# A hybrid decoder block: who issues the first small loads, and who sums the mixer's shift and scale

## The chip, the cores and the metric

The kernel runs on one core of a Trainium2 chip. The metric is device time in microseconds (us) of one execution. A core has five engines that run their own instruction streams in order: TensorE (PE, with its weight loads as PEld), VectorE (DVE), ScalarE (ACT), GpSimd (POOL) and SyncE (SP). Transfers between device memory and on-chip memory are issued by an engine's queue and carried out by 16 DMA engines.

## The reference

A decoder block over 2048 tokens of width 1024, all in float32. Cut to what matters here:

```
mod = c @ w_ada + b_ada                       # c: 1024 numbers, w_ada: 1024 x 6144
shift_m, scale_m, gate_m, shift_f, scale_f, gate_f = split(mod, 6)
h = rms_norm(x, g_pre_mix) * (1 + scale_m) + shift_m
proj = h @ w_in                               # q|k|v of attention, q|k|v|o, i|f of the mLSTM, gates
...                                           # sliding-window attention, chunkwise mLSTM, merge, w_out
x = x + gate_m * rms_norm(mix, g_post_mix)
...                                           # the same sandwich around a SwiGLU FFN
```

So nothing of the large products can start before the first columns of shift_m and scale_m (two products of the vector c with 1024 x 1024 matrices, 8 MB to read) are there.

## The kernel before

**Tiling.** The mixer goes over the sequence in four blocks of 512 tokens; the FFN follows in two halves. h is kept transposed: eight tiles k of 128 features by 512 tokens, each as a hi and a lo part (`hhi`, `hlo`), because each float32 product is made of three products in a faster format, hi·hi, hi·lo and lo·hi (`mm3`). Weights are loaded raw, 1 MB at a time (`raw`, two buffers), and each *piece* of a weight is split by `split`: ScalarE casts the hi part (`whi`, L256), VectorE subtracts to get the lo part (`wlo`, L257). The split tiles have four buffers, that is two pieces. `run` goes through a list of items; behind each piece it calls `advance`, which loads the next raw tile and splits pieces up to two ahead.

**Order.** The program is traced in one order. A planner then orders the instructions of each engine by a simulated timeline, by readiness and traced order, so an engine's final order may differ from the traced one. `tc.keep_in_program_order(i)` pins an instruction behind the one traced before it on its engine; `tc.issue_after(i)` puts what is traced inside it behind `i` on `i`'s engine. Neither adds a wait for another engine. Transfers wait for one of eight semaphores used in turn.

**The start.** SyncE issues x (two loads of 1 MB, `load_x`, L115), ten small loads (L142 to L153: biases, gains, convolution weights, positions, c, sinks), and w_ada in four chunks of 256 columns for shift and for scale (`load_ada`, L126, four loads of 512 KB for each chunk). Chunk 0 stands ahead of the first raw tile of the q weights (L288), chunks 1 and 2 ahead of the second, chunk 3 ahead of the k and v weights (L718). `hprep` squares x on ScalarE (L490), takes a root, scales x (L495 on ScalarE for the first block, L497 on VectorE for the others), and then, feature tile by feature tile, has TensorE transpose it (L209) and ScalarE write `hhi` (L504) and a copy (L506) with scale `s1` and bias `sh1`; GpSimd makes `hlo` (L507).

**Shift and scale.** `ada_first` handles a chunk: for each of eight k (rows p·8+k of w_ada), acc += c[k]·raw[k] on VectorE (L422 for the first k, L424 for the rest), for shift and scale; for chunk 0 the shift part is summed by TensorE instead, with c as a one-column weight. Matmuls with a column of ones (L204, `mix<-ones,tm`) sum over the partitions, and three small VectorE instructions (L444 to L446) add the bias and apply the gain. A chunk gives two feature tiles of h, which one piece of the q weights (`token_group`, four pieces of 24 products) multiplies. `rope_tables(0)` (L570 to L618, mostly VectorE) makes the tables that the rotary step behind q needs.

Of the kernel before, what the change touches and what calls it, by code (L numbers as in the profile page):

```python
# [2 lines left out]

# [1 line left out]

# [5 lines left out]
F32 = mybir.dt.float32  # L11
# [56 lines left out]
def decoder_block(ctx: ExitStack, tc: tile.TileContext, a: dict, out: bass.AP, dbg=None):  # L68
# [9 lines left out]
    small.tile([P, 8], F32, name="small_end", bufs=1)  # L78
# [24 lines left out]
    def tm(shape, dtype=F32):  # L103
        return mpool.tile(shape, dtype, tag="tm", name=nm("tm"), bufs=9)
# [8 lines left out]
    def load_x(src, big, i):  # L113
        xb = big([2, D])
        nc.sync.dma_start(xb, src[i * 256:(i + 1) * 256, :].rearrange("(t p) c -> p t c", p=P))  # L115
        return xb

    def load_ada(c0, n):

        kn = 2048 // n  # L120
        raws = {0: [], 1: []}
        for k0 in range(0, KD, 4):
            for part in (0, 1):
                if k0 % kn == 0:
                    raws[part].append(big([kn, n]))
                nc.sync.dma_start(raws[part][-1][:, k0 % kn:k0 % kn + 4, :],  # L126
                                  w_ada[:, part * D + c0:part * D + c0 + n].rearrange("(p k) c -> p k c", k=KD)[:, k0:k0 + 4, :])
# [6 lines left out]
    r0 = 0  # L134
    off = {}
# [9 lines left out]
    x_first.append(load_x(x_d, big, 1))  # L145
    posi = tm([S // P, P], I32)
    nc.sync.dma_start(posi, a["positions"].rearrange("o (t p) -> (o t) p", p=P))
    c_sb = const.tile([P, KD], F32, name="c_sb")
    nc.sync.dma_start(c_sb, a["c"].rearrange("o (p k) -> (o p) k", k=KD))
    b_if = const.tile([P, 8], F32, name="b_if")  # L150
    nc.sync.dma_start(b_if, a["b_if"].to_broadcast([P, 8]))
    sinks = const.tile([P, HQ], F32, name="sinks")
    nc.sync.dma_start(sinks, a["attn_sinks"].to_broadcast([P, HQ]))  # L153
    ada_raws = {c0: load_ada(c0, n) for c0, n, _ in ADA[:ADA_AHEAD[0]]}


    ident = const.tile([P, P], F32, name="ident")
# [38 lines left out]

    now = [0.0]
    streams = []

    def mm(o, lhsT, rhs, start, stop, resumed=False):  # L200

        n = int(np.prod(rhs.shape[1:]))
        now[0] += max(110.0, n * 0.422) if rhs.dtype == F32R else max(218.0, n * 1.7)
        T.matmul(o, lhsT=lhsT, rhs=rhs, start=start, stop=stop, skip_group_check=resumed)  # L204

    def transpose(o, i):
        now[0] += 110.0
# [36 lines left out]
    def split_tile(name):  # L244
        return wpool.tile([P, 1024], F32R, tag="split", name=nm(name), bufs=4)

    def split(src, shape, pair_heads=False, eng=V):
        n = int(np.prod(shape))
        hi, lo = split_tile("whi"), split_tile("wlo")
        hv = hi[:, :n].rearrange("p (k c) -> p k c", k=shape[0])  # L250
        lv = lo[:, :n].rearrange("p (k c) -> p k c", k=shape[0])
        if pair_heads:
            for k in range(shape[0]):
                sv = src[:, k, :].rearrange("p (g j d) -> p g j d", g=HKV, d=HD)
                hk, lk = (v[:, k, :].rearrange("p (j g d) -> p g j d", g=HKV, d=HD) for v in (hv, lv))
                A.copy(hk, sv)  # L256
                V.tensor_tensor(lk, sv, hk.bitcast(F32), op=ALU.subtract)  # L257
# [9 lines left out]
    class Piece:  # L267
        def __init__(self, raw, view, shape, mms, pair_heads=False):
            self.raw, self.view, self.shape, self.mms, self.pair_heads = raw, view, shape, mms, pair_heads
            self.wt = None  # L270
            raw.left += 1

    def mm3(ps, l, r, first, last):
# [68 lines left out]
    def run(items, between):  # L342
# [11 lines left out]
        def advance():  # L354
            nonlocal nload, nsplit
            while True:
                alive = sum(1 for r in raws[max(0, nload - 3):nload] if r.left)
                if nload < len(raws) and alive < 2:
                    between.get(nload, lambda: None)()
                    raws[nload].tile = raws[nload].load()  # L360
                    nload += 1
                    continue
                if nsplit < len(pieces) and nsplit < done + 2 and pieces[nsplit].raw.tile is not None:
                    p = pieces[nsplit]
                    p.wt = split(p.view(p.raw.tile), p.shape, p.pair_heads, G if nsplit < 3 else V)
                    p.raw.left -= 1
                    nsplit += 1
                    continue
                return

        advance()
        for it in items:
            if not isinstance(it, Piece):
                it()
                continue
            for _ in it.mms(it.wt):
                tick()
            tick()
            done += 1
            advance()  # L380
# [3 lines left out]
    s2 = const.tile([P, KD], F32, name="s2")  # L384
    b1 = const.tile([P, 48], F32, name="b1")
    V.tensor_scalar(b1, cols[:, off["b_ada"]:off["b_ada"] + 48], 1.0, None, op0=ALU.add)
    sh1 = const.tile([P, KD], F32, name="sh1")
    sh2 = const.tile([P, KD], F32, name="sh2")
    gg_m = mpool.tile([P, D], F32, name="gg_m")
# [33 lines left out]
            else:  # L423
                V.scalar_tensor_tensor(acc, raw[:, k, :], c_, acc, op0=ALU.mult, op1=ALU.add)  # L424

    def ada_first(c0, n, raws, on_pe):

        t0, nt = c0 // P, n // P
        acc = [tm([P, n]) for _ in range(2)]
        pt = mix_tile()  # L430
        ps = {part: mix_tile() for part in on_pe}
        for k in range(KD):
            for part in (0, 1):
                if part in on_pe:
                    mm(ps[part][0:1, :n], c_sb[:, k:k + 1], raws[part][k], k == 0, k == KD - 1)
                else:
                    ada_terms(acc[part], raws[part][k].unsqueeze(1), k, 1)
        for part in on_pe:
            A.copy(acc[part][0:1, :], ps[part][0:1, :n])
        for part in (0, 1):  # L440
            r = 1 if part in on_pe else P
            for j in range(nt):
                mm(pt[:, part * 8 + j:part * 8 + j + 1], acc[part][:r, j * P:(j + 1) * P], ones[:r, 0:1], True, True)
        V.tensor_tensor(sh1[:, t0:t0 + nt], pt[:, :nt], col("b_ada", t0, nt), op=ALU.add)  # L444
        V.tensor_tensor(s1[:, t0:t0 + nt], pt[:, 8:8 + nt], b1[:, 8 + t0:8 + t0 + nt], op=ALU.add)
        V.tensor_tensor(s1[:, t0:t0 + nt], s1[:, t0:t0 + nt], col("g_pre_mix", t0, nt), op=ALU.mult)  # L446

    def ada_stream(parts, gap):
        for part, kind in parts:
# [27 lines left out]
    def hprep(key, src, big, s_c, sh_c, first=False):  # L477
# [6 lines left out]
        for i in range(2):  # L484
# [6 lines left out]
            V.tensor_tensor(ss[:, 0:2], ss[:, 0:2], ss[:, 2:4], op=ALU.add)  # L491
            r = rsqrt_of_sumsq(ss[:, 0:2], 2)
            for t in range(2):
                if first:
                    A.activation(xb[:, t, :], xb[:, t, :], AF.Copy, scale=r[:, t:t + 1])  # L495
                else:
                    V.tensor_scalar(xb[:, t, :], xb[:, t, :], r[:, t:t + 1], None, op0=ALU.mult)  # L497
                xs.append(xb[:, t, :])
        yield L_X
        for k in range(KD):  # L500
# [145 lines left out]
    tables = {}  # L646

    def first_h(c0, n, on_pe):
        ada_first(c0, n, ada_raws[c0], on_pe)
        for _ in range(n // P):  # L650
            next(hp0)

    w_ba = a["w_branch_attn"][0]
# [2 lines left out]
    def block(b):  # L656
# [58 lines left out]

        def load_kv():
            raw = raw_tile([KD, 264])
            nc.sync.dma_start(raw[:, :, :256], w_in[:, C_K:C_K + 256].rearrange("(k p) c -> p k c", p=P))  # L718
# [960 lines left out]
```

## Time and profile before

| | |
|---|---|
| median of 3 runs | 2771.63 us (2771.41 to 2775.72) |
| profiled execution | 2771.54 us, span 2769.8 us |
| mean granted TensorE clock | 0.994 |
| PE busy | 2704.9 us (98%) |
| DVE busy | 1922.7 us (69%) |
| ACT busy | 1233.1 us (45%) |
| DMA | 402.63 MB, mean 145 GB/s |

Times in the profile count from the span's start. A row of the timeline has the start, the duration, engine, line, operation, what is written and read, and in brackets how long the engine had been idle and what ended that. A row of the waits has the waiter, the releaser, the sum, the number of times and the longest. A row of the windows has, for a stretch, its length, the busy time and the number of instructions of each engine, the granted TensorE clock, the DMA engines' busy share and the GB/s.

### The profile page before, as it was taken

To read this page: it belongs to the slowest core of one execution; us is meant where nothing else is said; L and a number is where in the kernel's file an instruction comes from. 1 tells how busy PE (TensorE), PEld (TensorE's weight loads), DVE (VectorE), ACT (ScalarE), POOL (GpSimd) and SP (SyncE) were. 2 spreads that over 40 slices of the span, in tenths; PEclk is the share of its full clock that TensorE was granted. 3 is DMA by queue.
4 is the path that set the end of the run, shared out by engine and by line. 5 is a ranking of instruction groups with operands and counts; after the bars stand their busy time and mean duration, and the time that the engine had idled before them with its cause. 6 is when DMAs were issued, how large, how long until landed. Compare 5 with 4: busy or idle time off the path is not lost.

```text
span 2769.8 us, 35110 instructions
## 1 busy us (share of the span) xinstructions
PE 2704.9 (98%) x12654; PEld 2199.7 (79%) x12654; DVE 1922.7 (69%) x3802; ACT 1233.1 (45%) x2285; POOL 153.1 (6%) x201
## 2 busy tenths in 40 slices
PE   6999999999999999999999999999999999999998
PEld 4778878788877888768887888887777888888886
DVE  7768657587674876657776777776676767666456
ACT  4543365433554335544363343334554333333444
POOL 2100001001010010110100000000000000000000
PEclk9999999999999999999999999999999999999999
DMA  7233353242552424523356555545666333233566
GB/s 236 88 111 103 100 180 123 80 137 80 169 163 65 135 86 139 180 67 97 98 168 216 172 176 181 175 152 194 203 236 210 130 102 108 98 111 131 189 212 213
DMA packets 280533, 402.63 MB, mean 145 GB/s; under 512 B 19220, under 2 KB 176536, under 8 KB 280360
## 3 DMA queue, kind: packets, MB, share of 16 engines
q1 hardware_dynamic: 280360, 400.40, 44.3%
q8 instruction: 99, 1.62, 0.2%
q14 instruction: 74, 0.61, 0.1%
HBM read 320.62 MB, written 79.73 MB: 145 GB/s over the span
## 4 chain that ended last, share of the span: by engine, by line
PE 87%; DVE 5%; DMA 4%; ACT 2%; issue 1%; POOL 0%; SPq 0%; DVEq 0%; POOLq 0%; ACTq 0%
PE acc L204 63%; PE mix L204 22%; PE mix L209 2%; DVE hl L1121 1%; DMA raw<-in_w_ffn_down_dram 1%; DVE tm L424 1%; DMA tx<-in_w_ada_dram 0%; ACT hl L1120 0%; DMA raw<-in_w_ffn_gate_dram 0%; DMA raw<-in_w_in_dram 0%; DMA raw<-as_d 0%; DMA x1n<-tx 0%; ACT big L1222 0%; POOL rs L472 0%; DMA w<-x 0%
## 5 line engine op out<-in xcount | busy, mean ns | idle before, releaser
L1120 ACT CAST hl<-raw 128x512 fp32r<-128x512 f32 x564 | 337.1, 620 | 400.2 <-PE mix L204 173.3
L1121 DVE TENSOR_TENSOR hl<-raw,hl 128x512 fp32r<-128x512 f32 x564 | 377.1, 687 | 169.5 <-ACT hl L1120 167.0
L259 ACT CAST whi<-raw 128x1024 fp32r<-128x1024 f32 (+1 forms) x208 | 212.1, 1020 | 501.0 <-PE acc L204 439.1
L260 DVE TENSOR_TENSOR wlo<-raw,whi 128x1024 fp32r<-128x1024 f32 (+1 forms) x208 | 247.4, 1189 | 181.0 <-ACT whi L259 178.2
L204 PE MATMUL acc<-hhi,wlo 128*128 128x512 f32 x896 | 353.9, 395 | 0.0
L204 PE MATMUL acc<-hhi,whi 128*128 128x512 f32 x896 | 352.4, 393 | 0.0
L204 PE MATMUL acc<-hlo,whi 128*128 128x512 f32 x896 | 351.8, 393 | 0.0
L204 PE MATMUL acc<-big,hl 128*128 128x512 f32 x1056 | 254.0, 389 | 0.6 <-ACT w L1328 0.6
L204 PE MATMUL acc<-hl,hl 128*128 128x512 f32 x1008 | 237.0, 393 | 6.9 <-DVE hl L1121 4.3
L204 PEld LDWEIGHTS acc<-big,hl 128*128 128x128 f32 x1056 | 198.0, 188 | 42.3 <-ACT w L1328 1.1
L204 PEld LDWEIGHTS acc<-hl,hl 128*128 128x128 f32 x1008 | 187.1, 188 | 52.6 <-DVE hl L1121 9.5
L204 PEld LDWEIGHTS acc<-hhi,wlo 128*128 128x128 f32 x896 | 168.3, 188 | 42.4 <-issue 8.1
L204 PE MATMUL mix<-big,hl 128*128 128x512 f32 x704 | 197.6, 392 | 3.2 <-DVE big L1257 3.2
L204 PEld LDWEIGHTS acc<-hlo,whi 128*128 128x128 f32 x896 | 168.3, 188 | 37.8 <-issue 3.2
L204 PEld LDWEIGHTS acc<-hhi,whi 128*128 128x128 f32 x896 | 168.4, 188 | 37.2 <-issue 4.1
L204 PE MATMUL mix<-hl,hl 128*128 128x512 f32 x792 | 182.4, 390 | 2.0 <-ACT hl L1120 1.3
L204 PEld LDWEIGHTS mix<-hl,hl 128*128 128x128 f32 x792 | 148.0, 188 | 35.5 <-DVE hl L1121 2.7
L204 PE MATMUL acc<-whi,big 128*128 128x512 f32 x512 | 166.0, 396 | 0.0
L204 PE MATMUL acc<-big,whi 128*128 128x512 f32 x512 | 158.4, 394 | 0.0
L204 PEld LDWEIGHTS mix<-big,hl 128*128 128x128 f32 x704 | 132.9, 189 | 32.0 <-DVE big L1257 4.4
L204 PE MATMUL acc<-whi,hhi 128*128 128x512 f32 (+1 forms) x384 | 133.3, 373 | 22.1 <-DVE tx L530 8.9
L204 PE MATMUL acc<-wlo,hhi 128*128 128x512 f32 (+1 forms) x384 | 140.7, 370 | 2.6 <-DVE wlo L260 2.6
(335 smaller groups left out, 4746.6 us busy)
## 6 DMA issues: line engine op xcount, KB each, us to landing
raw<-in_w_in_dram SPq DMA_DIRECT2D x76, 1024.0 KB, 5.1
as_d<-w SPq DMA_DIRECT2D x154, 256.0 KB, 2.2
raw<-as_d SPq DMA_DIRECT2D x70, 512.0 KB, 3.5
raw<-in_w_ffn_gate_dram SPq DMA_DIRECT2D x22, 1024.0 KB, 5.3
raw<-in_w_ffn_up_dram SPq DMA_DIRECT2D x22, 1024.0 KB, 6.3
raw<-ws_d SPq DMA_DIRECT2D x40, 512.0 KB, 4.3
tx<-in_w_ada_dram SPq DMA_DIRECT2D x64, 256.0 KB, 3.1
raw<-in_w_out_dram SPq DMA_DIRECT2D x16, 1024.0 KB, 5.1
```

Of the source, the lines that this page charges most:

```text
L204: T.matmul(o, lhsT=lhsT, rhs=rhs, start=start, stop=stop, skip_group_check=resumed)
L209: T.transpose(o, i, ident[:k, :k])
L259: A.copy(hv, src)
L260: V.tensor_tensor(lv, src, hv.bitcast(F32), op=ALU.subtract)
L424: V.scalar_tensor_tensor(acc, raw[:, k, :], c_, acc, op0=ALU.mult, op1=ALU.add)
L1120: A.copy(v(hi), src)
L1121: V.tensor_tensor(v(lo), src, v(hi).bitcast(F32), op=ALU.subtract)
```

## The change

- The ten small loads move from SyncE's to ScalarE's queue, c first; SyncE issues x, x, and chunk 0 at once.
- `ADA` now names, for each chunk, the k whose terms TensorE sums: all eight for chunk 0, k = 0 and 1 for the others. TensorE takes the raw w_ada tile as the weight and a column of c as the moving operand, so the result falls straight into the column that the partition sum goes to. VectorE sums k = 2 to 7 of chunks 1 to 3 (`ada_sums`), and the matmul with ones adds that to the same column.
- The bias and the gain are applied by ScalarE: two activations for each 128 columns, with `b1g` = (1 + b)·g made once.
- Chunk i + 1's matmuls and its two feature tiles are traced inside piece i, behind its sixth of eight `mm3` (a hook), and pinned there; the next product is queued behind the last of them. Chunks 2's and 3's VectorE sums are traced behind the piece before and pinned.
- For the first block x is scaled by VectorE too. The rope tables are traced behind chunk 3.

```diff
-ADA = [(0, 256, (0,)), (256, 256, ()), (512, 256, ()), (768, 256, ())]
+ADA = [(0, 256, tuple(range(8))), (256, 256, (0, 1)), (512, 256, (0, 1)), (768, 256, (0, 1))]
...
-    x_first = [load_x(x_d, big, 0)]
+    x_first = [load_x(x_d, big, i) for i in range(2)]
+    ada_raws = {c0: load_ada(c0, n) for c0, n, _ in ADA[:ADA_AHEAD[0]]}
+    c_sb = const.tile([P, KD], F32, name="c_sb")
+    nc.scalar.dma_start(c_sb, a["c"].rearrange("o (p k) -> (o p) k", k=KD))
...
-        nc.sync.dma_start(stack[r0:r0 + n, :], v)
+        nc.scalar.dma_start(stack[r0:r0 + n, :], v)
...
+    behind = []
     def mm(o, lhsT, rhs, start, stop, resumed=False):
...
-        T.matmul(o, lhsT=lhsT, rhs=rhs, start=start, stop=stop, skip_group_check=resumed)
+        with tc.issue_after(behind.pop().ins) if behind else nullcontext():
+            return T.matmul(o, lhsT=lhsT, rhs=rhs, start=start, stop=stop, skip_group_check=resumed)
...
-            for _ in it.mms(it.wt):
+            for n, _ in enumerate(it.mms(it.wt)):
                 tick()
+                if n == it.hook[0]:
+                    it.hook[1]()
...
+    def ada_sums(c0, n, on_pe):
+        rest = [k for k in range(KD) if k not in on_pe]
+        if not rest:
+            return
+        acc = ada_acc[c0] = [tm([P, n]) for _ in range(2)]
+        for k in rest:
+            for part in (0, 1):
+                c_, w_ = c_sb[:, k:k + 1], ada_raws[c0][part][k]
+                if k == rest[0]:
+                    i = V.tensor_scalar(acc[part], w_, c_, None, op0=ALU.mult)
+                else:
+                    i = V.scalar_tensor_tensor(acc[part], w_, c_, acc[part], op0=ALU.mult, op1=ALU.add)
+                if c0 > ADA[1][0]:
+                    tc.keep_in_program_order(i)
+    def ada_first(c0, n, on_pe):
+        t0, nt = c0 // P, n // P
+        acc = ada_acc.get(c0)
         pt = mix_tile()
...
+        for part, k in sorted(((part, k) for k in on_pe for part in (0, 1)), key=lambda z: (z[1] // 4, z)):
             for j in range(nt):
+                i = mm(pt[:, part * 8 + j:part * 8 + j + 1], ada_raws[c0][part][k][:, j * P:(j + 1) * P], c_sb[:, k:k + 1],
+                       first, k == KD - 1, resumed=True)
+                first = False
+                if c0:
+                    tc.keep_in_program_order(i)
+        if acc:
+            for j in range(nt):
+                for part in (0, 1):
+                    i = tc.keep_in_program_order(mm(pt[:, part * 8 + j:part * 8 + j + 1], acc[part][:, j * P:(j + 1) * P],
+                                                    ones[:, 0:1], False, True, resumed=True))
+            behind[:] = [i]
+        for j in range(nt):
+            t = t0 + j
+            A.activation(sh1[:, t:t + 1], pt[:, j:j + 1], AF.Identity, bias=col("b_ada", t))
+            A.activation(s1[:, t:t + 1], pt[:, 8 + j:9 + j], AF.Identity, scale=col("g_pre_mix", t), bias=b1g[:, t:t + 1])
+            yield
...
-                if first:
-                    A.activation(xb[:, t, :], xb[:, t, :], AF.Copy, scale=r[:, t:t + 1])
-                else:
-                    V.tensor_scalar(xb[:, t, :], xb[:, t, :], r[:, t:t + 1], None, op0=ALU.mult)
+                V.tensor_scalar(xb[:, t, :], xb[:, t, :], r[:, t:t + 1], None, op0=ALU.mult)
...
     def program():
-        for i, ch in enumerate(ADA):
-            if i == 3:
+        items = [it for b in range(NBLK) for it in block(b)]
+        yield lambda: ada_sums(*ADA[1])
+        yield lambda: first_h(*ADA[0])
+        for i in range(len(ADA)):
+            if i + 1 < len(ADA):
+                if i:
+                    yield lambda ch=ADA[i + 1]: ada_sums(*ch)
+                items[0].hook = 5, lambda ch=ADA[i + 1]: first_h(*ch)
+            else:
                 yield lambda: tables.update({0: rope_tables(0)})
-            yield lambda ch=ch: first_h(*ch)
-        items = [it for b in range(NBLK) for it in block(b)]
+            yield items.pop(0)
```

Two small pins are left out above: the first two pieces' lo parts are queued behind `b1g` on VectorE, and the first load of the k and v weights behind the last load of w_ada.

More of the change, by code (lines that the diff above doesn't have):

```diff
@@ L1 @@
 import math
-from contextlib import ExitStack
+from contextlib import ExitStack, nullcontext
 import numpy as np
@@ L77, in decoder_block @@
     small = ctx.enter_context(tc.tile_pool(name="small", bufs=2))
-    small.tile([P, 8], F32, name="small_end", bufs=1)
     wpool = ctx.enter_context(tc.tile_pool(name="wpool", bufs=2))
@@ L141, in decoder_block @@
                        ("norm_w", a["mlstm_norm_w"].rearrange("o (t p) -> (o t) p", p=P), 4)):
-        nc.sync.dma_start(stack[r0:r0 + n, :], v)
+        nc.scalar.dma_start(stack[r0:r0 + n, :], v)
         off[name] = r0
         r0 += n
-    x_first.append(load_x(x_d, big, 1))
     posi = tm([S // P, P], I32)
-    nc.sync.dma_start(posi, a["positions"].rearrange("o (t p) -> (o t) p", p=P))
-    c_sb = const.tile([P, KD], F32, name="c_sb")
-    nc.sync.dma_start(c_sb, a["c"].rearrange("o (p k) -> (o p) k", k=KD))
+    nc.scalar.dma_start(posi, a["positions"].rearrange("o (t p) -> (o t) p", p=P))
     b_if = const.tile([P, 8], F32, name="b_if")
-    nc.sync.dma_start(b_if, a["b_if"].to_broadcast([P, 8]))
+    nc.scalar.dma_start(b_if, a["b_if"].to_broadcast([P, 8]))
     sinks = const.tile([P, HQ], F32, name="sinks")
-    nc.sync.dma_start(sinks, a["attn_sinks"].to_broadcast([P, HQ]))
-    ada_raws = {c0: load_ada(c0, n) for c0, n, _ in ADA[:ADA_AHEAD[0]]}
+    nc.scalar.dma_start(sinks, a["attn_sinks"].to_broadcast([P, HQ]))
     ident = const.tile([P, P], F32, name="ident")
@@ L245, in split_tile, with split @@
         return wpool.tile([P, 1024], F32R, tag="split", name=nm(name), bufs=4)
-    def split(src, shape, pair_heads=False, eng=V):
+    def split(src, shape, pair_heads=False, first=False):
         n = int(np.prod(shape))
@@ L256, in split @@
                 A.copy(hk, sv)
-                V.tensor_tensor(lk, sv, hk.bitcast(F32), op=ALU.subtract)
+                with tc.issue_after(b1g_made.ins) if first else nullcontext():
+                    V.tensor_tensor(lk, sv, hk.bitcast(F32), op=ALU.subtract)
         else:
@@ L364, in advance @@
                     p = pieces[nsplit]
-                    p.wt = split(p.view(p.raw.tile), p.shape, p.pair_heads, G if nsplit < 3 else V)
+                    p.wt = split(p.view(p.raw.tile), p.shape, p.pair_heads, nsplit < 2)
                     p.raw.left -= 1
@@ L386, in decoder_block @@
     V.tensor_scalar(b1, cols[:, off["b_ada"]:off["b_ada"] + 48], 1.0, None, op0=ALU.add)
+    b1g = small.tile([P, KD], F32, name="b1g", bufs=1)
+    b1g_made = V.tensor_tensor(b1g, b1[:, 8:16], cols[:, off["g_pre_mix"]:off["g_pre_mix"] + KD], op=ALU.mult)
     sh1 = const.tile([P, KD], F32, name="sh1")
@@ L648, in first_h @@
     def first_h(c0, n, on_pe):
-        ada_first(c0, n, ada_raws[c0], on_pe)
-        for _ in range(n // P):
+        for _ in ada_first(c0, n, on_pe):
             next(hp0)
```

32 lines of the change are left out of this document (9 added, 23 removed).

## The prediction

> **What bounds the kernel now.** I read the spans first, then the windows, the waits, the timeline and chain of the first 90 us, and the DMA view. The windows decide where to look:
>
> ```profile
> core 0: 2769.8 us, clock 0.994
> core 0: us, PE busy (x) PEld busy (x) DVE busy (x) ACT busy (x) POOL busy (x), PEclk, DMA share, GB/s
> 0.00:24.70 24.70, 8.28 (x34) 3.92 (x34) 10.34 (x36) 13.88 (x28) 3.89 (x45) 1.00 0.88 293
> 24.70:57.60 32.90, 26.18 (x120) 21.06 (x120) 32.42 (x83) 10.41 (x17) 8.16 (x6) 0.84 0.71 228
> 57.60:65.00 7.40, 7.36 (x24) 5.53 (x24) 6.57 (x16) 3.36 (x6) 2.57 (x2) 0.77 0.36 116
> 65.00:77.00 12.00, 10.47 (x78) 9.50 (x78) 11.77 (x30) 6.16 (x11) 0.00 (x0) 1.00 0.33 100
> 77.00:90.00 13.00, 11.61 (x70) 10.04 (x68) 10.07 (x42) 7.40 (x16) 1.29 (x4) 1.00 0.55 183
> 90.00:2769.80 2679.80, 2641.02 (x12334) 2149.68 (x12332) 1851.49 (x3599) 1191.85 (x2210) 137.14 (x144) 1.00 0.44 143
> ```
>
> Behind 90 us TensorE is busy 2641.02 of 2679.80 us at full clock: what it gains in front, it keeps to the end. In front it is idle 16.4 us up to its first product at 24.7, then 6.7, 0.0, 1.5 and 1.4 us, and from 24.7 to 65 the granted clock is 0.84 and 0.77. Between 24.7 and 57.6 VectorE is full (32.42 of 32.90). The waits and the timeline say what TensorE waited for:
>
> ```profile
> ACT hhi L504 <- DVE s L446: 22.8, 4, 10.6
> PE acc L204 <- ACT hhi L504: 8.6, 3, 3.2
> 21.41 2.18 ACT L256 CAST whi<-raw 128x512 fp32r<-128x512 f32 x4 [1.21 <-DMA raw<-in_w_in_dram]
> 24.75 0.54 PE L204 MATMUL acc<-whi,hhi 128*128 128x512 f32 x1 [2.53 <-ACT hhi L504]
> 38.09 0.79 PE L204 MATMUL acc<-whi,hhi 128*128 128x512 f32 x1 [3.24 <-ACT hhi L504]
> 53.00 0.50 PE L204 MATMUL mix<-ones,tm 128*128 128x1 f32 x4
> 56.23 0.15 DVE L444 TENSOR_TENSOR sh<-mix,cols 128x2 f32<-128x2 f32 x1
> 56.81 0.78 ACT L504 ACTIVATE hhi<-mix,sh,s 128x512 fp32r<-128x512 f32 x1 [6.55 <-DVE s L446]
> 57.64 0.50 PE L204 MATMUL acc<-whi,hhi 128*128 128x512 f32 x1 [2.87 <-ACT hhi L504]
> ```
>
> Each h chunk waits for VectorE: for its 16 sums, and then for its three small finishing operations in VectorE's queue. For the last chunk TensorE's partition sums are through at 53.5, and L444 comes at 56.23. The last piece of the q projection starts at 57.64.
>
> **The loads.** The queue's issues, and the DMA rates in slices of 1.5 us:
>
> ```profile
> 0.80 1.28 ACT L490 ACT_TABLE_LOAD   x1 [0.80 <-PEq L1669]
> 0.80 4.85 DMA big<-in_x_dram
> 6.97 0.43 SPq L153 DMA_DIRECT2D sinks<-in_attn_sinks_dram  x1
> 7.44 2.89 SPq L126 DMA_DIRECT2D big<-in_w_ada_dram  x4
> 8.68 0.63 ACT L490 ACTIVATE tx<-big 128x512 f32<-128x512 f32 x1 [0.45 <-DMA big<-in_x_dram]
> 10.38 11.01 DMA raw<-in_w_in_dram
> GB/s 0 131 421 367 404 123 51 290 355 367 355 378 378 353 348 348 349 347 348 348 360 378 375 354 348 348 350 355 223 26 0 0 0 0 0 0 113 378 208 0
> ```
>
> From 12 us on, the pipe is full at about 350 GB/s, hence 6.0 us for a chunk's 2.1 MB and 3.0 us for half of the q weights; between 7.5 and 10.5 us (123, 51) it is nearly empty, because chunk 0 was issued only at 7.44, behind ten small loads. Off SyncE, chunk 0 follows x: x by 8.7 as now, chunk 0 by 14.7, the first q weights by 17.7 instead of 21.4. That is 3.7 us; the hole's missing bytes alone (227+299 GB/s over 1.5 us each, by 350) give 2.3, the moved issue 5.6: these are its bounds. The estimated landings, before and after: chunk 1 27.4, 23.7; chunk 2 33.4, 29.7; second q weights 36.4, 32.7; chunk 3 42.4, 38.7. ScalarE pays ten issues of 0.43, 4.7 us with their gaps, ahead of squares that start at 5.67, when x has landed. With its table load of 1.28 it is free at 6.8, late by 1.1 us; I cost it at nothing, since x is ready by 14 to 15 and chunk 0's sums are later.
>
> **Prices.** The rows for the pieces that follow:
>
> ```profile
> 6.21 0.19 ACT L490 ACTIVATION_READ_ACCUMULATOR tx<-big 128x1 f32 x1
> 11.15 4.25 ACT L495 ACTIVATE big<-big,rs 128x1024 f32<-128x1024 f32 x4
> L497 DVE TENSOR_SCALAR big<-big,rs x12: 746/748/754, 352.6 to 1071.8; 128x1024 f32<-128x1024 f32 x12
> 21.71 0.50 PE L204 MATMUL mix<-ones,tm 128*128 128x1 f32 x4
> 32.87 1.07 PE L209 MATMUL mix<-ident,big 128*128 128x128 f32 x8
> 33.33 2.85 DVE L424 SCALAR_TENSOR_TENSOR tm<-big,c_sb,tm 128x256 f32<-128x256 f32 x7
> 22.06 0.69 DVE L257 TENSOR_TENSOR wlo<-raw,whi 128x512 fp32r<-128x512 f32 x1 [1.32 <-ACT whi L256]
> 25.09 0.63 PE L204 MATMUL acc<-wlo,hhi 128*128 128x512 f32 x1
> 25.51 0.63 PE L204 MATMUL acc<-whi,hhi 128*128 128x512 f32 x1
> 31.04 1.07 PE L204 MATMUL acc<-whi,hlo 128*128 128x512 f32 x4
> 38.79 1.57 DVE L424 SCALAR_TENSOR_TENSOR tm<-big,c_sb,tm 128x256 f32<-128x256 f32 x1
> 47.05 0.28 DVE L570 TENSOR_TENSOR tx<-inv_freq,pos 128x128 f32<-128x128 f32 x1
> 65.69 0.29 DVE L614 SCALAR_TENSOR_TENSOR tx<-tx 128x128 f32<-128x128 f32 x1
> ```
>
> A one-column matmul with 128 weight columns costs 0.13 us (four in 0.50), a transpose 0.13, a VectorE sum 0.41, a weight's hi part 0.55 (four in 2.18), its lo part 0.6 at the pitch of that engine. A product starts every 0.23 us warm and every 0.42 (25.09 to 25.51) at half clock. The new small ScalarE finish is bounded by the 0.19 and the 0.78 rows; I take 0.25, near the 128x1 row, so 0.5 for the two that a transposed chunk waits for. VectorE's x scaling costs 4 times 0.75, while ScalarE loses 4.25 us; x is then ready between 14 and 15.
>
> **The change, step by step.**
>
> Chunk 0: no VectorE sums. When the last quarter lands at 14.7, 8 matmuls remain (1.0), then 0.5 and one h tile (0.78): 17.0. The q weights at 17.7 plus a cast make the first product 18.4, against 24.75. TensorE has then waited 2.6 us; the trace shows half clock behind waits of 2.53 and 2.87, so I charge 8 products at 0.42 and 10 at 0.23: 5.7, to 24.1. The Trainium skill ("TensorE: Matmul & The Clock Gate", What's actually happening) has the clock fall only after an idle window of about 3.4 us; by that this piece would be 1.5 us shorter, but the trace's waits were under it and still paid.
>
> Chunk 1, inside piece 0 behind 18 of 24 products: it landed at 23.7, and 7 of the 12 remaining sums need the last quarter: 2.9, to 26.6. TensorE's eight matmuls end at 25.1; it waits 1.5, sums 0.5. Then 6 products and 8 transposes (2.4) cover ScalarE's 1.3: piece 1 at 29.5, against 38.09.
>
> Chunk 2: the program traces the split of piece 2's weights ahead of these sums and pins the first sum behind it. So they start after the second q weights, 32.7, two casts 1.1 and a lo part 0.6: 34.4, though their data is there at 29.7. Twelve sums are 4.9, plus one hold of 1.1 (1.57 against about 0.48 while GpSimd works on hlo): 40.4. TensorE is at the pinned matmuls at 33.7, done with eight at 34.7, and waits 5.7: half clock again. Sums to 40.9, then 6 products at 0.42 and the transposes: piece 2 at 44.4.
>
> Chunk 3: piece 3's split needs piece 1's two weight buffers, free at 43.4; two casts and a lo part, 45.1; sums with a hold, 51.1. TensorE comes at 48.5, ends its eight at 49.5, waits 1.6, and starts piece 3 at 54.0 instead of 57.64: 3.6 us. The piece then runs warm, 5.6 against 7.4 us: 1.8 more, 5.4 at the end of q.
>
> The rope tables (35 operations, L570 to L614, at some 0.25: 8.8 us) are what VectorE does in its gaps, 26.6 to 33.8 and 40.4 to 44.5; in the trace before they lie between 47 and 66, mixed with chunk 3's sums. That cover costs up to 4.7 if it is gone (below). VectorE sheds 8 + 12 sums (8.2) and 12 small finishes (about 1.2), and takes 3.0 for x: 6.4 less, so of TensorE's idle 2.9 us from 65 to 90, where VectorE is busy 11.77 of 12, I count 2.1 as gained. Together 5.4 + 2.1 = 7.5 us.
>
> The profiled execution is 2771.54 us: the span of 2769.8 and 1.7 around it; the median of the runs is 2771.63, the same. So 2771.5 − 7.5 = **2764.0 us**. Its own uncertainty is 3 us: the load hole (2.3 to 5.6) and the two half-clock windows (1.6 each).
>
> **Rivals.**
>
> *No hold on VectorE.* If piece 2's lo parts don't stand in front of chunk 2's sums, they end at 32.6, before TensorE arrives; piece 2 starts at 37.5, chunk 3's sums at 41.6, piece 3 at 45.7, q ends at 51.3, 13.7 earlier. The rope tables then have no gap and give back some 3: 11 us, 2760.5. For it: VectorE's order is a planner's, not the program's. Against: the explicit pin. Chance 0.2.
>
> *Rope tables in the wrong gap.* Placed whole between chunk 2's sums and piece 3's split, 8.8 us fill a gap of 4.1: chunk 3 is 4.7 later, piece 3 at 58.7. Of the gain only the later idle remains, with the earlier tables: some 2 us, 2769.5. For it: they float freely. Chance 0.15.
>
> *Slower: VectorE's pinned chain behind an unmoved load.* The small loads share the pipe, the hole persists in another place, and the second q weights land at 36.4 as now. Then in one string: two casts and lo 38.1, sums 44.1, rope tables with two holds 55.1, split 56.3, sums 62.3, 2.9 to the next product: 65.2 against 57.64, 7.6 slower; the saved idle gives back nothing as VectorE is later too: 2779. It decides from 60.0 on (2 us of warm clock given). Beside it: the Trainium skill ("Trainium Kernel Development and Optimization", Key Constraints) says that queues of several engines run on the same 16 DMA engines and save issue time alone; the row with 123 and 51 says that issue time was what was missing. Chance 0.1.
>
> *It doesn't reach the end:* TensorE arrives earlier at the attention of block 0 and waits there for VectorE; within 1 us of before, 2771. Chance 0.05.
>
> **How the numbers follow.** The forecast has 0.5, its own range 2761 to 2767. 0.2% is 5.5 us, about what a measurement here can tell. Faster by more: 0.82 of 0.5 and all of 0.2, 0.61. Same: 0.08 of the forecast, 0.15 and 0.05, 0.28. Slower 0.1 and a rest, 0.11. A range of 2758.5 to 2770.0 holds the first three cases and leaves out the other two and the tails.
>
> **What would show it.** First product near 18.4, piece 1 near 29.5, piece 2 near 44, piece 3 near 54; no DMA hole behind x; VectorE idle or on rope between 27 and 33; ScalarE with eight short finishes per part and no wait on VectorE's L446. Wrong if piece 2 starts before 40 or piece 3 after 57, or if squares start after 7 us because ScalarE's issues wait.

## The result: 0.7% slower, and where the profile puts it

| | before | after |
|---|---|---|
| median (runs) | 2772.54 us (6; 2771.04 to 2775.72) | 2793.7 us (6; 2790.74 to 2795.21) |
| ratio | | 1.0073 [1.006, 1.0086] |
| profiled execution, span | 2771.54, 2769.8 us | 2795.21, 2793.5 us |

The change costs 21.2 us where 7.5 were forecast as gained. The windows of the changed kernel, cut as those of before:

```profile
core 0: us, PE busy (x) PEld busy (x) DVE busy (x) ACT busy (x) POOL busy (x), PEclk, DMA share, GB/s
0.00:24.70 24.70, 1.15 (x5) 0.85 (x5) 8.46 (x28) 8.36 (x21) 3.89 (x45) 1.00 0.96 325
24.70:57.60 32.90, 32.83 (x166) 29.82 (x167) 9.79 (x24) 8.28 (x18) 5.16 (x4) 1.00 0.55 175
77.00:90.00 13.00, 5.11 (x27) 3.97 (x26) 10.71 (x37) 3.34 (x6) 0.03 (x1) 0.81 0.44 130
90.00:2793.50 2703.50, 2663.91 (x12464) 2168.85 (x12464) 1867.99 (x3660) 1202.94 (x2233) 137.74 (x148) 1.00 0.45 143
```

TensorE does almost nothing up to 24.7 us (1.15 us against 8.28 before), is then busy without a pause up to 57.6, and stands still for 7.9 us between 77 and 90. VectorE, full between 24.7 and 57.6 before, has 9.79 of 32.9 us to do. A warning for the column PEclk: this trace holds no clock record before 44.2 us, and the column reads 1.00 there; the pitch of the matmuls below says otherwise.

For the comparisons below I number the wide products (matmuls into `acc`) of TensorE in each trace, and call a *lag* by how much later than in the trace of before one of them starts; each trace is one execution. Lag of the changed kernel: +15.2 us at the first product, +15.4 at the last of the q projection (80.0 against 64.6), +21.8 at the 350th (158 against 136 us); behind that it stays between 18.3 and 23.5 to the end. So the loss has two parts: 15 us ahead of the first product and some 7 behind q.

**Ahead of the first product.** ScalarE's queue and engine in the timeline:

```profile
0.80 0.43 ACTq L134 DMA_DIRECT2D c_sb<-in_c_dram  x1
2.34 0.31 ACTq L145 DMA_DIRECT2D tm<-in_g_pre_ffn_dram  x1
6.20 0.32 ACTq L145 DMA_DIRECT2D tm<-in_conv_w_dram  x1
7.52 0.32 ACTq L149 DMA_DIRECT2D tm<-in_positions_dram  x1
11.97 0.39 ACTq L151 DMA_DIRECT2D b_if<-in_b_if_dram  x1
12.40 0.49 ACTq L153 DMA_DIRECT2D sinks<-in_attn_sinks_dram  x1
12.92 1.28 ACT L517 ACT_TABLE_LOAD   x1 [12.92 <-DMA tm<-in_positions_dram]
14.21 0.63 ACT L517 ACTIVATE tx<-big 128x512 f32<-128x512 f32 x1
```

Each issue takes 0.3 to 0.6 us, as forecast; but between the fourth and the fifth lie 3.5 us, and between the eighth and the ninth 4.1. The eight transfer semaphores go round over both queues: `conv_w` comes to the one of x's first half, which lands at 6.2, and `b_if` to that of `conv_w`. The DMA view gives `conv_w`'s time from issue to landing, and the rates of the first 60 us in slices of 1.5:

```profile
tm<-in_conv_w_dram ACTq DMA_DIRECT2D x1, 16.0 KB, 5.7
GB/s 0 98 388 423 423 358 344 341 346 370 380 280 379 355 348 349 346 348 350 369 386 359 349 92 287 378 354 335 25 11 0 0 0 0 5 0 0 0 5 0
```

16 KB need 5.7 us in a pipe that is now full of x and w_ada: no packet of ScalarE's queue starts between 6.98 and 9.92 us. (The hole at 7.5 to 10.5 us is gone, as forecast.) ScalarE waits inside its instruction stream, and its squares start at 14.21 instead of 5.67 us. What hangs on them, on VectorE and TensorE:

```profile
18.07 1.42 DVE L521 TENSOR_SCALAR big<-big,rs 128x1024 f32<-128x1024 f32 x2 [0.90 <-POOL rs L499]
21.90 0.28 DVE L181 COPY cols<-mix 128x128 f32<-128x128 f32 x1
23.73 0.21 DVE L187 CAST tm<-tm 16x128 f32<-16x128 int32 x1
24.00 0.28 PE L189 MATMUL mix<-ident,tm 16*128 16x16 f32 x1 [10.93 <-DVE tm L187]
24.21 13.81 PE L205 MATMUL mix<-c_sb,big 128*128 128x1 f32 x64
38.22 0.34 ACT L472 ACTIVATE s<-mix,b1g,cols 128x1 f32<-128x1 f32 x1
39.91 0.79 PE L205 MATMUL acc<-whi,hhi 128*128 128x512 f32 x1
46.11 1.84 PE L205 MATMUL mix<-c_sb,big 128*128 128x1 f32 x16
```

VectorE can scale x only from 18.07 on. The cast of the positions, which needs nothing of x, is behind that in its order; their transpose (L189) waits for the cast, and chunk 0's sums are behind the transpose on TensorE. They are 64 instructions, two for each float32 matmul, that start every 0.213 us, 13.8 us in all; the 16 of chunk 1, behind wide products, start every 0.112.

**Behind q.** The waits of the first 100 us, and the place itself:

```profile
DVE wlo L259 <- ACT whi L257: 28.1, 2, 23.0
PE mix L205 <- DVE tm L446: 1.3, 2, 0.9
PE acc L205 <- ACT tm L698: 8.2, 2, 7.9
```

```profile
88.78 0.23 DVE L637 TENSOR_SCALAR tx<-tx 128x128 f32<-128x128 f32 x1
89.04 0.31 ACT L641 ACTIVATE sin<-tx 128x128 f32<-128x128 f32 x1 [7.10 <-DVE tx L637]
89.68 1.05 ACT L698 COPY tm<-acc 128x512 f32<-128x512 f32 x2
90.30 0.59 PE L205 MATMUL acc<-whi,hhi 128*128 128x264 f32 x1 [7.88 <-ACT tm L698]
```

The rope tables stand behind all of VectorE's sums in its order, 70.9 to 89.3 us, although it had been idle for 23 us between 30 and 53. ScalarE's sine waits for them, q's copies out of `acc` (L698) are behind the sine, and TensorE waits for these copies until 90.3.

### The profile page after: what moved, and what is told of

Read it like the earlier page. It is cut to its first block, busy times and chain, and to the rows that moved or that the text cites. A ratio compares the mean times of both kernels' runs of the same rounds, so it can differ in the third digit from the quotient of the medians.

```text
span 2793.5 us, 35268 instructions
## 1 busy us (share of the span) xinstructions
PE 2721.1 (97%) x12742; PEld 2218.2 (79%) x12742; DVE 1908.5 (68%) x3775; ACT 1231.6 (44%) x2296; POOL 151.9 (5%) x201
## 4 chain that ended last, share of the span: by engine, by line
PE 86%; DVE 5%; DMA 4%; ACT 2%; issue 1%; POOL 0%; SPq 0%; ACTq 0%; DVEq 0%; POOLq 0%
PE acc L205 63%; PE mix L205 22%; PE mix L210 2%; DVE hl L1145 1%; DMA w<-x 1%; DMA raw<-as_d 1%; ACT hl L1144 1%; DMA raw<-in_w_ffn_gate_dram 0%; POOL rs L499 0%; DMA ws_d<-big 0%; ACT big L1246 0%; DVE w L1502 0%; DMA raw<-in_w_ffn_down_dram 0%; DVE tm L446 0%; DVE wlo L259 0%
## 5 line engine op out<-in xcount | busy, mean ns | idle before, releaser
L205 PE MATMUL acc<-hhi,wlo 128*128 128x512 f32 x896 | 353.9, 395 | 0.0
L205 PE MATMUL acc<-hhi,whi 128*128 128x512 f32 x896 | 352.5, 393 | 0.0
L205 PE MATMUL acc<-hlo,whi 128*128 128x512 f32 x896 | 352.0, 393 | 0.0
L205 PE MATMUL acc<-big,hl 128*128 128x512 f32 x1056 | 254.0, 389 | 0.8 <-ACT w L1357 0.5
L205 PE MATMUL acc<-hl,hl 128*128 128x512 f32 x1008 | 237.4, 393 | 6.6 <-DVE hl L1145 4.6
L205 PEld LDWEIGHTS acc<-big,hl 128*128 128x128 f32 x1056 | 198.0, 188 | 42.9 <-ACT w L1352 1.1
L205 PEld LDWEIGHTS acc<-hl,hl 128*128 128x128 f32 x1008 | 186.9, 188 | 52.8 <-DVE hl L1145 9.8
L205 PEld LDWEIGHTS acc<-hhi,wlo 128*128 128x128 f32 x896 | 168.3, 188 | 41.4 <-issue 7.3
L205 PE MATMUL mix<-big,hl 128*128 128x512 f32 x704 | 197.6, 392 | 2.6 <-DVE big L1281 2.6
L205 PEld LDWEIGHTS acc<-hlo,whi 128*128 128x128 f32 x896 | 168.3, 188 | 38.7 <-issue 4.1
L205 PEld LDWEIGHTS acc<-hhi,whi 128*128 128x128 f32 x896 | 168.4, 188 | 37.1 <-issue 4.1
L205 PE MATMUL mix<-hl,hl 128*128 128x512 f32 x792 | 182.5, 391 | 1.8 <-DVE ms L497 0.9
L205 PEld LDWEIGHTS mix<-hl,hl 128*128 128x128 f32 x792 | 147.7, 188 | 35.6 <-DVE hl L1145 3.1
L205 PE MATMUL acc<-whi,big 128*128 128x512 f32 x512 | 166.0, 396 | 0.0
L205 PE MATMUL acc<-big,whi 128*128 128x512 f32 x512 | 158.3, 394 | 0.0
L205 PEld LDWEIGHTS mix<-big,hl 128*128 128x128 f32 x704 | 132.8, 189 | 31.3 <-DVE big L1281 3.8
L205 PE MATMUL acc<-whi,hhi 128*128 128x512 f32 (+1 forms) x384 | 132.9, 374 | 19.6 <-ACT tm L698 10.9
L205 PE MATMUL acc<-wlo,hhi 128*128 128x512 f32 (+1 forms) x384 | 140.4, 369 | 0.2 <-DVE wlo L262 0.2
```

The source lines that it names most:

```text
L205: return T.matmul(o, lhsT=lhsT, rhs=rhs, start=start, stop=stop, skip_group_check=resumed)
```

## The experiments

Theories, as the expectations name them. **A**: ScalarE's waits on its loads delay the squares and all that follows. **B**: one-column matmuls leave TensorE at half clock, so 64 of them cost twice what was counted. **C**: the rope tables at the end of VectorE's order cost the 7.9 us behind q. **D**, as forecast: the pinned sums of chunks 2 and 3 hold pieces 2 and 3. The results, with the positions of the first product (P1) and the start of q's last one, and the lag at the 350th:

| kernel | median, us | ratio to before | P1 | q's last | lag 350 |
|---|---|---|---|---|---|
| before | 2772.2 to 2773.7 | | 24.7 | 64.6 | 0 |
| after | 2793.7 | 1.0073 [1.006, 1.0086] | 39.9 | 80.0 | +21.8 |
| b1_loads_act | 2780.31 | 1.0027 [1.0018, 1.0036] | 32.6 | 71.3 | +7.8 |
| e1_sync_loads | 2786.03 | 1.005 [1.0035, 1.0065] | 30.1 | 71.8 | +14.1 |
| e3_rope_early | 2782.3 | 1.0039 [1.0024, 1.0053] | 39.2 | 79.3 | +11.8 |
| g0_sync_rope | 2777.85 | 1.0019 [1.001, 1.0028] | 30.4 | 72.6 | +5.2 |
| e6_warm | 2797.72 | 1.0088 [1.0071, 1.0105] | 43.6 | 84.8 | +27.0 |
| g1_sync_rope_c0 | 2780.88 | 1.0025 [1.0014, 1.0035] | 25.4 | 68.4 | +2.2 |
| e4_unpin | 2792.33 | 1.0073 [1.0058, 1.0088] | 39.7 | 77.9 | +20.7 |
| h1_sync_rope_c0_unpin | 2773.48 | 1.0003 [0.9993, 1.0012] | 25.1 | 63.6 | −2.6 |
| k1_spread | 2771.74 | 0.9994 [0.9985, 1.0003] | 25.1 | 60.2 | −3.7 |
| k3_all | 2775.27 | 1.0007 [0.9998, 1.0016] | 27.1 | 62.8 | −3.3 |

**The loads, both ways.** `b1_loads_act` is the kernel before with the load part of the change alone; `e1_sync_loads` is the changed kernel with the loads back in before's order:

```diff
# e1_sync_loads (b1_loads_act is the reverse, on the kernel before)
-    x_first = [load_x(x_d, big, i) for i in range(2)]
-    ada_raws = ...
-    nc.scalar.dma_start(c_sb, ...)            # and stack, positions, b_if, sinks
+    x_first = [load_x(x_d, big, 0)]           # then stack; x's second half; positions, c, b_if, sinks
+    nc.sync.dma_start(c_sb, ...)              # all on SyncE
+    ada_raws = ...                            # behind them
```

> The kernel before with the load part of the change alone: x twice, chunk 0 and then the rest on SyncE, the ten small loads on ScalarE. Theory A: ScalarE's squares start near 14 and its scaling of x ends near 24; first product near 33 instead of 24.75; VectorE's sums, which run on meanwhile, give part of it back by the last chunk: 2 to 8 us slower than before, about 2777. Rival (the loads are harmless or help by the 3.7 us of the forecast): within 1 us of before or faster.

> The changed kernel with the ten small loads, the second load of x and chunk 0 back on SyncE in the order of before; all else as changed. Theory A (ScalarE's issues wait for semaphores whose small loads take some 5 us each to land, so the squares start at 14.2 instead of 5.7, and x, the bias columns and the position cast, behind which TensorE's first sums stand, are late): squares at 5.7, chunk 0's sums start at 14 as their data lands and take 64 times 0.213 us, first product near 29.5 instead of 39.9, time about 10 us less, 2783. Rival (the start is late because of chunk 0's sums themselves or of VectorE's order, whoever issues the loads): first product stays behind 36, time within 4 us of 2793.

```profile
11.63 1.28 ACT L489 ACT_TABLE_LOAD   x1 [11.63 <-DMA tm<-in_mlstm_norm_w_dram]
12.93 0.63 ACT L489 ACTIVATE tx<-big 128x512 f32<-128x512 f32 x1
32.57 0.80 PE L203 MATMUL acc<-whi,hhi 128*128 128x512 f32 x1 [4.16 <-ACT hhi L503]
```

That is `b1_loads_act`: squares at 12.93, the first product 7.8 us late (6.7 at q's last), the median 8.1 us above that of before in the same round of runs; 2 to 8 were expected. In `e1_sync_loads` the sums start when their data lands, and the first product comes 9.8 us earlier than in the changed kernel:

```profile
13.96 3.55 PE L206 MATMUL mix<-c_sb,big 128*128 128x1 f32 x16 [4.46 <-DMA big<-in_w_ada_dram]
18.25 10.24 PE L206 MATMUL mix<-c_sb,big 128*128 128x1 f32 x48
30.15 0.80 PE L206 MATMUL acc<-whi,hhi 128*128 128x512 f32 x1 [0.70 <-ACT hhi L529]
```

Theory A holds from both sides: the load part alone costs 8.1 us, and taking it back gives 7.7 (10 were expected). Both runs move the queue and the order of the loads together; that it is ScalarE's stream that waits is read from the rows above, and in `e1_sync_loads` the squares start at 5.88. The sums are still 13.8 us long, and the first product is 5.4 us later than before.

**The rope tables.** `e3_rope_early` traces them behind chunk 0's two tiles of h instead of behind chunk 3; `g0_sync_rope` has this and the loads on SyncE.

```diff
# e3_rope_early
         yield lambda: first_h(*ADA[0])
+        yield lambda: tables.update({0: rope_tables(0)})
...
-            else:
-                yield lambda: tables.update({0: rope_tables(0)})
```

> The changed kernel with the rope tables traced behind chunk 0's h tiles instead of behind chunk 3. Theory C (the tables, now last on VectorE before q's rotary step, hold ScalarE's sine and cosine and behind them the copies of q's PSUM banks, for which TensorE waits 7.9 us at 82): tables done before 45, TensorE's wait gone, 8 us less, 2786. Rival (the wait only moves: VectorE's splits and the sums of chunks 2 and 3 come later by as much): less than 3 us gained.

> The changed kernel with both repairs at once: small loads back on SyncE, rope tables traced behind chunk 0's h tiles. If the two causes are separate (theories A and C), their gains add: 2793.7 - 7.7 - 11.4 = 2774.6, first product near 30, TensorE's wait on the q copies under 1 us, and what is left above the kernel before (some 2 us) is chunk 0's 64 one-column matmuls. Rival: with the loads early, VectorE is busy with rope tables when chunk 1's sums come, so they only trade places: 2778 to 2782, as each repair alone.

```profile
PE acc L205 <- ACT tm L698: 0.3, 1, 0.3
```

In `e3_rope_early` the wait of 7.9 us is 0.3, and the time falls by 11.4: theory C, with a larger price than the wait alone. The clock has the rest. These are the products 109 to 130, behind the wait, in the changed kernel and then in `e3_rope_early`:

```profile
90.30:95.30 5.00, 5.00 (x22) 5.00 (x23) 5.00 (x14) 1.02 (x2) 0.00 (x0) 0.50 0.29 96
81.57:84.25 2.68, 2.68 (x24) 2.68 (x23) 2.68 (x7) 0.58 (x1) 0.00 (x0) 1.00 0.09 31
```

In the changed kernel the clock is at half from 85.2 to 95.4 us, which makes these products 2.3 us longer. The gain of `e3_rope_early` is 0.7 us at q's last product, 8.7 at the first behind the wait, 11.0 behind the half clock, and 10.0 at the 350th.

In `g0_sync_rope` both repairs give 15.9 together, 3.2 less than their sum; but before ran 1.2 us slower in its round than in that of the single repairs, and the intervals of the ratios are 2.5 us and more to each side, so that the difference is not clear of noise. Against before it is 4.4 us slower, where some 2 were expected. Its 49th product starts at 56.1, later than in `e1_sync_loads` (52.3): piece 2's lo parts, ahead of the pinned sums, waited there 4.06 us for their cast, up to 45.84, and the clock was at half from 52.7 to 59.5. The runs do not separate the two.

**One-column matmuls and the clock.** `e6_warm` puts 16 wide products into a spare bank ahead of chunk 0's sums:

```diff
# e6_warm, in ada_first
+        if c0 == 0:
+            for _ in range(16):
+                w_ = T.matmul(wps, lhsT=wt[:, :P], rhs=wt, start=True, stop=True)   # wt: a piece's hi part
+            behind[:] = [w_]
```

> The changed kernel with sixteen wide products (128x512, the first part of the q weights with itself, into a PSUM bank that nobody reads) on TensorE right in front of chunk 0's one-column sums; they add work and change no result. Theory B (one-column matmuls run at half clock because they don't raise TensorE's clock, however many follow each other): the sums start every 0.11 us instead of every 0.213, 64 of them in about 7.2 instead of 13.7 us; the sixteen cost 5 to 7 us, so that the first product comes at about the same 39 to 40, and piece 0 is warm from its start (1.5 us less): time 2792. Rival (a one-column matmul on w_ada's tiles costs 0.213 us for another reason, such as transfers into on-chip memory at the time): the pitch stays 0.21 and the time is 5 to 7 us longer.

```profile
24.12 6.57 PE L460 MATMUL mix<-whi 128*128 128x512 f32 x16
30.53 11.17 PE L206 MATMUL mix<-c_sb,big 128*128 128x1 f32 x64
```

```profile
29.80:33.20 3.40, 3.40 (x29) 3.24 (x27) 0.07 (x1) 0.00 (x0) 0.00 (x0) 1.00 1.06 373
33.20:46.90 13.70, 13.62 (x57) 12.57 (x57) 0.00 (x0) 3.68 (x8) 2.55 (x2) 0.50 0.64 198
```

The expected 7.2 us are not reached: the 64 take 11.2 instead of 13.8, the first product comes at 43.6 instead of 39 to 40, and the kernel is no faster. The windows say why. The wide products bring the clock up for 29.8 to 33.2 us; in that time TensorE does little else than one-column matmuls, and the clock goes back to 0.50 for the next 13.7, though TensorE is busy 13.62 of them (with one-column matmuls up to 41.5, then transposes, and products from 43.6 on). So a long row of one-column matmuls neither raises the clock nor keeps it. The rival, transfers at the same time, falls: the first 25 of the 64 start every 0.112 us with the DMA share at 1.06, the others every 0.213 with 0.64. The Trainium skill ("TensorE: Matmul & The Clock Gate", What's actually happening) has the gate go by how busy the array has been, and fall after an idle window of about 3.4 us; the length of the window agrees with the traces, but here it fell in a stretch that the profile counts as busy.

`g1_sync_rope_c0` shortens the sums instead: chunk 0 as the other chunks, on `g0_sync_rope`.

```diff
-ADA = [(0, 256, tuple(range(8))), ...
+ADA = [(0, 256, (0, 1)), ...
...
+        yield lambda: ada_sums(*ADA[0])
         yield lambda: ada_sums(*ADA[1])
```

> As the run before it, and chunk 0 summed as the other chunks: part k 0 and 1 by TensorE (16 one-column matmuls instead of 64), the rest by VectorE. Theory B (one-column matmuls at half clock, 0.213 us each, are what delays the first product to 30): 48 fewer are 10.2 us of TensorE, VectorE's 12 sums cost 4.9 behind the last landing, so the first product is at 25 to 26 and the time 4 us less, 2770.5. Rival (pieces behind the first are bound by weight buffers and by the pinned sums of chunks 2 and 3 on VectorE): first product earlier, the end of q the same, time within 1 us of the run before it.

The first product moves from 30.4 to 25.4 and q's end by 4.2, as expected; the lag at the 350th falls by 3.0 only, and the median does not fall (the two intervals overlap), so neither the forecast of 4 us less nor the rival's unmoved end of q came. The largest wait left inside q is for chunk 2's pinned sums:

```profile
47.78 1.87 PE L206 MATMUL mix<-ones,tm 128*128 128x1 f32 x8 [4.56 <-DVE tm L447]
```

**The pins.** `h1_sync_rope_c0_unpin` takes the pins off VectorE's sums on `g1_sync_rope_c0`; `e4_unpin` does the same on the changed kernel alone.

```diff
-                if c0 > ADA[1][0]:
-                    tc.keep_in_program_order(i)
```

> As the run before it, without the pins on VectorE's sums of chunks 2 and 3, which then stand in front of piece 2's lo parts in VectorE's order. Theory D (the pinned sums behind the lo parts hold pieces 2 and 3, VectorE being idle in front of them): pieces 2 and 3 start 3 to 5 us earlier each, time 2766 to 2768. Rival (the lo parts wait for piece 0's buffers and TensorE reaches the sums late anyhow): piece 2 earlier by under 1 us, time within 1 us of the run before it.

> The changed kernel without the pins alone. Theory D: in the changed kernel VectorE is idle between 30 and 53 us and does chunk 2's sums only at 54.9 to 59.1, behind lo parts that waited 23 us for buffers. Without the pin they are done when TensorE comes; piece 2 starts at 55 to 56 instead of 60.2, piece 3 follows some 4 us earlier; the wait for the q copies behind the rope tables stays at about 8: 2789. Rival: nothing, 2793, because the split buffers hold pieces 2 and 3.

On the repaired kernel theory D holds: that wait is gone, the 49th product starts at 47.7 instead of 52.2, the 73rd at 58.4 instead of 62.8, and the time is 7.4 us less (4.8 of them are there at the 350th product), level with before but not the 2766 to 2768 us that were expected. In the changed kernel alone, D fails: the 49th starts 0.3 us earlier, the 73rd 2.0, and the time is 1.4 less, within the noise. There TensorE comes so late that the sums keep it waiting 0.9 us at most, as the row `L205 <- DVE tm L446` above says.

**Spreading the one-column matmuls.** In `h1_sync_rope_c0_unpin` two windows of q are at half clock, and each begins inside a block of 24 one-column matmuls and eight transposes in a row: the 3.41 us in front hold 2.6 and 2.5 us of one-column matmuls. The same block for chunk 1, 31.8 to 35.2, lies across two such windows, with 2.1 and 0.5 us of them, and is followed by none here; in `k3_all` it lies in one, with 2.4 us, and half clock follows at 35.8. So here it depends on where the block falls.

```profile
44.15:47.56 3.41, 3.41 (x13) 2.93 (x12) 3.41 (x10) 3.41 (x8) 1.23 (x1) 0.50 0.05 12
54.39:57.80 3.41, 3.41 (x14) 3.12 (x15) 0.00 (x0) 2.98 (x8) 0.56 (x1) 0.50 0.80 258
```

`k1_spread` puts the matmuls of chunks 2 and 3 with c in fours between the products of the piece, and the transposes come between products too. `k3_all` adds an earlier chunk 0 and five wide products in front of the first real one.

```diff
# k1_spread
-                items[0].hook = 5, lambda ch=ADA[i + 1]: first_h(*ch)
+                # chunks 2, 3: a quarter of the matmuls with c behind mm3 0, 1, 2 and 3, the rest behind 4
# k3_all
+    ada_raws = ...          # ahead of positions, b_if, sinks; behind c
...
+            if c0 == 0:     # behind chunk 0's sums
+                for _ in range(5):
+                    i = T.matmul(wps, lhsT=wt[:, :P], rhs=wt, start=True, stop=True)
```

> The last variant (loads on SyncE, rope tables early, chunk 0 as the others, no pins on VectorE), with the one-column matmuls and transposes of chunks 2 and 3 spread between the products of the piece in front instead of in one block of 3.4 to 4 us. Theory B (a window of 3.4 us filled by one-column matmuls and transposes makes the next window run at half clock): the windows at half clock from 44.15 and from 54.39 us vanish, 13 products are 0.2 us shorter each, q ends 2.4 us earlier, 2771. Rival (the clock falls for another reason): the windows stay, q ends as before, 2773.5 within 1 us.

> As the run before it, chunk 0's loads issued ahead of positions, b_if and sinks (c stays ahead), and five wide products into a spare bank between chunk 0's sums and the first product, where TensorE waits 2.35 us. Theory: first product 1.3 us earlier, near 23.8, and the clock up one window earlier (1.5 us): 2768 to 2769, below the kernel before. Rival (the wide products only delay the real ones, or the clock stays down as the window before is not full; the load order is hidden behind VectorE's sums): first product 25 or later, 2771 to 2773.

```profile
36.00:45.20 9.20, 9.20 (x57) 7.79 (x55) 9.10 (x24) 4.08 (x11) 2.78 (x2) 1.00 0.92 281
45.20:54.70 9.50, 9.47 (x58) 7.94 (x57) 8.51 (x21) 6.55 (x14) 3.10 (x2) 1.00 0.00 1
54.70:60.20 5.50, 5.50 (x23) 4.31 (x24) 0.54 (x2) 2.88 (x5) 2.59 (x2) 1.00 0.98 331
```

In `k1_spread` the same work, spread, keeps the clock at 1.00 up to q's end, which comes 3.4 us earlier (2.4 were expected); a half-clock window follows at 66.0, behind q, and of the 3.4 us 1.1 are left at the 350th product. Its time cannot be told from before's. `k3_all` is no better, against its forecast of 2768 to 2769:

```profile
16.13 0.28 PE L190 MATMUL mix<-ident,tm 16*128 16x16 f32 x1 [8.52 <-DVE tm L188]
16.35 3.57 PE L207 MATMUL mix<-c_sb,big 128*128 128x1 f32 x16
22.87 2.48 PE L485 MATMUL mix<-whi 128*128 128x512 f32 x5
25.15 1.91 PE L214 MATMUL mix<-ident,big 128*128 128x128 f32 x8
27.13 0.80 PE L207 MATMUL acc<-whi,hhi 128*128 128x512 f32 x1
```

The positions now land late, their transpose stands in front of chunk 0's matmuls again, the planner has put all eight transposes behind the wide products, and the first product is 2.0 us later than in `k1_spread`.

**What stays open.** `h1`, `k1` and `k3` lead by 2.6 to 3.7 us at the 350th product and have lost it at the end of the profiled executions. The lead comes and goes in steps of 1 to 3 us, some at windows of 3.41 us at half clock that each trace, before's too, has at other places (before at 407, 1121, 1479 and 1486 us), some between 2555 and 2695 us, where no trace has a window at half clock. The runs of before themselves spread over 7 us. A gain of 3 us at the front is thus not settled by these runs, and neither is why `g1_sync_rope_c0` loses 5 us more behind the 350th product than it lagged there. No run gives the small loads to a third queue, GpSimd's, or puts all of them behind chunk 0 on SyncE.

## Why the prediction was wrong, by its own steps

**"ScalarE pays ten issues of 0.43 … late by 1.1 us; I cost it at nothing": failed.** The issues were counted as 4.7 us of work. They took 12.1 us, since an issue waits for its semaphore, and the semaphore for a transfer; the squares were 8.5 us late. The rows that could have warned stood in the trace of before:

```profile
3.57 0.40 SPq L115 DMA_DIRECT2D big<-in_x_dram  x1
5.67 0.32 SPq L147 DMA_DIRECT2D tm<-in_positions_dram  x1
```

SyncE issues positions, its ninth transfer, only when x's first half has landed, 1.7 us after it was free. The hole in the pipe was in part that wait, not the ten issues alone, and the change moved it onto an engine with work to do. The text's own mark, squares behind 7 us, came true.

**"8 matmuls remain (1.0)" at 14.7: failed three ways.** They started at 24.2 (+9.5, through squares, x's scaling, the cast of the positions and their transpose); there were 64 instead of 8, since none had been done before and each of 32 float32 matmuls is two instructions; and each took 0.213 instead of 0.13 us: 13.8 against 1.0 (+12.8). The ending was 0.8 shorter than forecast. In sum +21.5: 39.9 for 18.4. The price was misread: the row's four in 0.50 us are four instructions, so two float32 matmuls. That rows of one-column matmuls run at half clock could not be read from four of them behind wide products, but one row of before shows both the doubling and the slow start:

```profile
14.21 5.58 PE L204 MATMUL mix<-big,c_sb 128*1 128x256 f32 x16 [4.79 <-DMA big<-in_w_ada_dram]
```

Eight float32 products of c are 16 instructions here, and they start every 0.43 us up to 18.2 us and every 0.22 behind it.

**Pieces 1 to 3.** Forecast 41 us from the first product to the end of q, measured 40.1, against 39.9 before. So what the new order gains inside q is nothing here. Chunk 2's "waits 5.7: half clock again" didn't come (0.94 us), for TensorE was late; with the front repaired it did, at 4.56 us in `g1_sync_rope_c0`, and taking off the pins repaid it. The step was right for a kernel that this one was not.

**"The rope tables … are what VectorE does in its gaps, 26.6 to 33.8 and 40.4 to 44.5 … That cover costs up to 4.7 if it is gone": failed.** The gap was there and larger (23 us), but the planner left the tables where they were traced, behind all sums. The price is not that VectorE is late for sums, as the rival had it, but ScalarE's sine in front of q's copies: 7.9 us of wait and 2.3 of half clock behind it, 11.4 in the time. So the 2.1 us that were counted as gained behind q became a loss of 6.4 (lag +15.4 at q's last product, +21.8 at the 350th). The rival put them into another gap and still forecast a gain of 2 us; it had neither the place nor the waiter.

**The loads' landing** was right: the hole went (423, 358, 344 GB/s where 123 and 51 stood), and chunk 0 was there at 14.96 us and the first q weights at 17.79, where 14.7 and 17.7 were forecast. The 3.7 us that this was to bring reached nothing: q's weights were cast from 19.13 instead of 21.41, and TensorE had nothing to multiply them with for 20 us. The Trainium skill ("Trainium Kernel Development and Optimization", Key Constraints), named in the slower rival, counts issue time as all that a second queue saves. Here it saved nothing in the end: the issues waited in ScalarE's own stream, and `b1_loads_act` is 8.1 us slower.

The slower rival put the loss in chunk 3's string on VectorE, 7.6 us; the loss is three times that and lies in front of it and behind it.

## What to carry to other kernels

Before a load is moved to another engine's queue, look at what its issue waits for, not how long it takes: a full pipe turned ten issues of 0.4 us into 12 us of an engine that had work. When work is moved from one engine to another, count its instructions on the new engine and price them at the clock that this very work gives: here 64 one-column instructions in a row cost 0.213 us each, and 24 of them with eight transposes were in three places followed by 3.41 us at half clock, while in fours between wide products they left the clock at 1.00. And follow each step that the change traces later through every in-order engine behind it; here a sine that nobody wanted yet held the copies that all waited for.

## What the runs showed that I had not expected

- TensorE busy with a long row of one-column matmuls is at half clock: one every 0.213 us against 0.112, and 16 wide products raise the clock for one window of 3.4 us only. A block of 24 of them with transposes between wide products was followed by 3.41 us at 0.50 where one such window held 2.4 to 2.6 us of its one-column matmuls, and not where they were split into 2.1 and 0.5.
- 16 KB take 5.7 us from issue to landing while megabytes fill the same 16 DMA engines.
- The removal of the same pins gave 7.4 us in the repaired kernel and nothing clear of noise in the changed one: what a step costs depends on what comes before it.
